# A two-layer encoder trunk on one core: separate PSUM banks and a fixed order at the stage borders, another beginning, and the pooling map moved one step forward

## The chip, the cores and the metric

The kernel runs on one core of one Trainium2 chip. The metric is the time of one execution on the device in microseconds (us); the median of three runs stands for a kernel. The engines named below are TensorE (PE, matrix products, with its weight loads PEld), VectorE (DVE), ScalarE (ACT), GpSimd (POOL) and SyncE (SP), which issues most of the transfers. PSUM is the memory that PE writes its results to; it has eight banks, each of 512 fp32 columns in 128 partitions.

## The reference

An input x of 256 tokens and 1024 channels passes two layers. Each layer does three things to it, all in fp32:

```
for l in range(2):
    x = x + 0.5 * swiglu(rmsnorm(x, ffn1_norm[l]), w_gate, w_up, w_down)     # 1024 -> 2816 -> 1024
    z = rmsnorm(x, mix_norm[l]) @ w_in[l]
    zq, zk, zv, zp, hq, hi, hff, hfb, hg = split(z)
    y_att  = dilated_attention(zq, zk, zv, ...)      # 8 heads of 64
    y_pool = pool_mixer(zp, pool_w[l], pool_scale[l])    # window means, a 64x64 map per group, a scale
    y_rec  = hgrn2_bidirectional(hq, hi, hff, hfb, hg, ...)
    x = x + concat(y_att, y_pool, y_rec) @ w_out[l]
    x = x + 0.5 * swiglu(rmsnorm(x, ffn2_norm[l]), w_gate, w_up, w_down)
```

The pooling map and its scale, `y_pool`, and the way x gets from one of the six stages to the next are what the change touches, beside the beginning.

## The kernel before, in words

**Products.** Each fp32 operand is split into a high part and a low part, and each product is three matmuls (high by high, low by high, high by low; lines 161 to 163 and 168 to 170). Weights come from memory in halves of 128x1024 (`stage`, SP's queue); ACT copies the high part (`whi`, line 149) and DVE subtracts to get the low part (`wlo`, line 150), four halves ahead of PE's use. One half feeds twelve matmuls of 512 columns or 24 of 256.

**Stages.** A layer is feed-forward 1, mixer, feed-forward 2. In a feed-forward, each of eleven blocks computes gate and up (`gu`), `g` on ACT and `h` on DVE, transposes h on PE (`hp`) and multiplies it into four accumulators `ya`, one for each half of the channels (dh) and of the tokens (tt). PE and SP follow the order of the program; ACT, DVE and POOL follow an order that a scheduler makes from it. In the mixer a table, ORDER, sets the order of steps: `c:n` takes a quarter chunk of the input projection, `rec` the recurrence's last products (`ops`), `sc`, `tr` and `pv` the attention, `pool` the pooling map (`pps`, then the parts `yh` on ACT and `yl` on DVE), and `o:` the output projection (`wo`), whose first part, `o:pool/0`, reads `yh` and `yl`.

**A border.** There are five borders, where a stage's result is added to x and becomes the next stage's input. At the end of a stage the last block of each (dh, tt) is a run of six matmuls; then DVE adds it to x (`add`, line 371), ACT sums its squares (`squares`, line 281), and, one run later, PE transposes that quarter of x by four transposes (`turn`, line 294) into PSUM tiles named `xps`. After both token halves ACT makes the high part `xh` (line 272) and DVE the low part `xl` (line 273) of each of four channel chunks k. An `xps` tile is one bank that holds two chunks. The last quarter's transposes are held back (`pending`) and run by `late_turn`: in a feed-forward ahead of the second weight half, in the mixer's first products (`proj_pair`) after 24 matmuls.

**PSUM.** The eight banks are two pools of four, `pg` (gate and up, hp, xps, most of the mixer's short-lived results) and `py` (the accumulators `ya`, and the output projection's).

**The beginning.** While the first transfers are under way PE does twelve idle products of a tile of ones; each is two passes in the trace. Then it transposes the first half of x, and the second half after the first weight half.

Of the kernel before, what the change touches and what calls it, by code (L numbers as in the profile page):

```python
# [16 lines left out]
P = 128  # L17
D = 1024
T = 256
KC = D // P  # L20
# [21 lines left out]
HALF = 1024  # L42
# [6 lines left out]
    (  # L49
# [4 lines left out]
    ),  # L54
    (
# [4 lines left out]
    ),  # L60
)
# [9 lines left out]
class Trunk:  # L71
    def __init__(self, ctx, tc, x_in, wall, prm_in, rel_in, cst_in, cst2_in, msk_in, band_in, y_out):
# [16 lines left out]
        self.n_split = 0  # L89
        self.cur = 0  # L90
        self.pending = self.then = None
        self.look = LOOK

        self.x = self.cp.tile([P, 2, D], F32, name="x")
# [27 lines left out]
        self.eps, self.one = (cols[:, n:n + 1] for n in range(2))  # L122
# [19 lines left out]
    def split_part(self, i, c0, c1):  # L142
        nc = self.nc
        self.feed_dma(i)
        if c0 == 0:
            self.split_t[i] = (self.whl.tile([P, HALF], F32R, tag="hi", name="whi"),
                               self.whl.tile([P, HALF], F32R, tag="lo", name="wlo"))
        (hi, lo), st, s = self.split_t[i], self.stage_t[i], slice(c0, c1)
        nc.scalar.activation(hi[:, s], st[:, s], AF.Copy)  # L149
        nc.vector.tensor_tensor(lo[:, s], st[:, s], hi[:, s].bitcast(F32), op=ALU.subtract)  # L150

    def ahead(self, i):

# [49 lines left out]
    def proj_pair(self, i0, accs, mid=None):  # L203

        self.ahead(i0)
        ws = [self.half(i0 + n, KC) for n in range(4)]
        order = [(kc, n) for kc in range(4) for n in range(4)] + [(kc, n) for n in range(4) for kc in range(4, KC)]
        for kc, n in order:
            if (kc, n) == (2, 0):
                self.late_turn()  # L210
            if (kc, n) == (KC - 1, 1) and mid is not None:
                mid()
            wh, wl = ws[n]
            self.mm3(accs[n // 2][:, n % 2, :], wh[:, kc, :], wl[:, kc, :], self.xh[:, kc, :], self.xl[:, kc, :],
                     start=(kc == 0 and n % 2 == 0), stop=(kc == KC - 1 and n % 2 == 1))
# [20 lines left out]
    def down(self, i, ys, ah, al, first, last, mid=None, post=None, dhs=(0, 1)):  # L236

        for dh in dhs:
            self.ahead(i + dh)
            wh, wl = self.half(i + dh, 2)  # L240
            for tt in range(2):
                s = slice(tt * P, tt * P + P)
                for f in range(2):
                    self.mm3t(ys[2 * dh + tt], ah[:, f, s], al[:, f, s], wh[:, f, :], wl[:, f, :],
                              start=(first and f == 0), stop=(last and f == 1))
                if post is not None:
                    post(dh, tt)
            if dh == 0 and mid is not None:
                mid()

# [11 lines left out]
    def new_xt(self):  # L262
# [2 lines left out]
        self.ss = self.wk.tile([P, 64], F32, tag="ss", name="ss", bufs=2)[:, 0:4]  # L265
        self.xps = {}

    def parts(self, stage, k, src):

        nc = self.nc  # L270
        g = self.prm[:, C_GAIN + stage * 8 + k:C_GAIN + stage * 8 + k + 1]
        nc.scalar.activation(self.xh[:, k, :], src, AF.Copy, scale=g)  # L272
        nc.vector.scalar_tensor_tensor(self.xl[:, k, :], src, g, self.xh[:, k, :].bitcast(F32),  # L273
                                       op0=ALU.mult, op1=ALU.subtract)

    def squares(self, stage, dh, tt):

# [9 lines left out]
    def turn(self, stage, dh, tt):  # L287

        nc = self.nc
        for j in range(4):  # L290
            k = 4 * dh + j
            if tt == 0 and j % 2 == 0:
                self.xps[k // 2] = self.pg.tile([P, 2, T], F32, tag="g", name="xps")
            nc.tensor.transpose(self.xps[k // 2][:, j % 2, tt * P:tt * P + P], self.x[:, tt, k * P:k * P + P], self.ident)  # L294
        if tt == 1:
            for k in range(4 * dh, 4 * dh + 4):
                self.parts(stage, k, self.xps[k // 2][:, k % 2, :])

    def rms(self, rows=False):

# [67 lines left out]

    def add(self, y, by, dh, tt, post):
        s = self.x[:, tt, dh * 512:dh * 512 + 512]  # L370
        self.nc.vector.scalar_tensor_tensor(s, y, by, s, op0=ALU.mult, op1=ALU.add)
        post(dh, tt)

    def to_stage(self, stage):
# [77 lines left out]
    def mixer(self, l):  # L452
# [4 lines left out]
        V = {}  # L457
# [4 lines left out]
        def bank(name):  # L462
            return pg.tile([P, 2, T], F32, tag="g", name=name)
# [281 lines left out]
            nc.scalar.activation(pm, ps, AF.Copy)  # L745

        def pool_out():
            ps = bank("pps")
            for n in range(2):
                c = C_PW + (2 * l + n) * P  # L750
                nc.tensor.matmul(ps[:, n, :], lhsT=self.prm[:, c:c + P], rhs=V["pm"][:, n, :], start=(n == 0),
                                 stop=(n == 1), skip_group_check=True)
            yh, yl = V["ypool"] = self.t2("yh", F32R), self.t2("yl", F32R)
            for n in range(2):
                sc = self.prm[:, C_PS + 2 * l + n:C_PS + 2 * l + n + 1]
                nc.scalar.activation(yh[:, n, :], ps[:, n, :], AF.Copy, scale=sc)
                nc.vector.scalar_tensor_tensor(yl[:, n, :], ps[:, n, :], sc, yh[:, n, :].bitcast(F32),
                                               op0=ALU.mult, op1=ALU.subtract)


# [51 lines left out]
    def body(self):  # L812
        nc = self.nc
        self.new_xt()

        idle = self.pg.tile([P, 512], F32, tag="g", name="idle")
        for _ in range(12):
            self.nc.tensor.matmul(idle[:, 0:P], lhsT=self.ones, rhs=self.ones, start=True, stop=True)
        for j in range(2):
            self.split_part(0, j * HALF // 2, (j + 1) * HALF // 2)  # L820
        self.n_split = 1
        for tt in range(2):
            self.turn(0, 0, tt)
        self.feed_dma(5)

        def second():
# [1 line left out]
                self.turn(0, 1, tt)  # L828

        def sums():  # L830
            for dh in range(2):
                for tt in range(2):
# [138 lines left out]
```

## Time and profile before

| | |
|---|---|
| median of three runs (lowest, highest) | 1016.76 us (1016.58, 1017.47) |
| profiled execution, its own time | 1017.16 us |
| its span | 1015.4 us |
| PE busy | 1002.1 us (99%) |
| DVE busy | 607.6 us (60%) |
| ACT busy | 539.2 us (53%) |
| granted clock of TensorE, mean | 0.999 |
| memory read | 179.15 MB |

The span runs from the first to the last instruction of the profiled execution; its own time is 1.8 us longer. A row of a timeline gives the start of an instruction in us from the span's start, how long it took (for x4, from the first one's start to the last one's end), its engine, line, operation and shape, and in brackets the idle time of the engine just before it with what ended it. Matmuls overlap: a matmul of 512 columns is shown with 0.39 us, but such matmuls start 0.23 us apart, so a busy engine can still be late, and a recorded wait is shorter than the time lost by it.

### The profile page before, as it was taken

Reading aid. Unit: us, or ns where it says so; the run is one execution under the profiler, and the core shown is the slowest. Engines: PE = TensorE matmul, PEld = TensorE weight load, DVE = VectorE, ACT = ScalarE, POOL = GpSimd, SP = SyncE. Lnnn points to the kernel's source line nnn. Section 1 sums busy time; section 2 is a strip of 40 time slices with the busy share of each in tenths; the row PEclk is TensorE's granted clock in tenths of the full one; section 3 lists DMA queues with packets and bytes.
Section 4 is the critical chain, followed back from the end, with each engine's and each line's share of the span. In section 5 each row is a group of like instructions: output and inputs, shape, how many; then the busy total and the mean of one; then the engine's idle time right before and its main releaser. Section 6 shows DMA issues by size and latency. Waiting matters only on the chain.

```text
span 1015.4 us, 14477 instructions
## 1 busy us (share of the span) xinstructions
PE 1002.1 (99%) x5722; PEld 827.2 (81%) x5722; DVE 607.6 (60%) x811; ACT 539.2 (53%) x774; POOL 3.3 (0%) x8
## 2 busy tenths in 40 slices
PE   9999999999999999999999999999999999999998
PEld 7888788798877888888878888888888778888886
DVE  5555555679865555555565454546998665545453
ACT  7444444675765544444474444446857764444441
POOL 0000100000000000000000000000000000000000
PEclk9999999999999999999999999999999999999999
DMA  7676775544434556555655565654553356555661
GB/s 265 216 259 189 265 271 187 170 163 147 127 104 146 184 186 190 187 187 186 188 165 188 187 188 186 189 185 144 186 154 117 106 146 186 188 187 187 189 189 56
DMA packets 50276, 181.16 MB, mean 178 GB/s; under 512 B 5752, under 2 KB 6008, under 8 KB 49952
## 3 DMA queue, kind: packets, MB, share of 16 engines
q1 hardware_dynamic: 48528, 174.09, 53.9%
q0 software_dynamic: 720, 4.21, 1.1%
q10 hardware_dynamic: 960, 1.94, 0.5%
q8 instruction: 45, 0.74, 0.3%
q14 instruction: 23, 0.19, 0.0%
HBM read 179.15 MB, written 3.16 MB: 180 GB/s over the span
## 4 chain that ended last, share of the span: by engine, by line
PE 93%; ACT 3%; DVE 3%; DMA 1%; issue 0%; SPq 0%; ACTq 0%
PE gu L168 16%; PE gu L170 16%; PE gu L169 16%; PE ya L170 8%; PE ya L168 8%; PE ya L169 8%; PE hp L352 2%; PE lev L544 1%; PE wo L168 1%; PE wo L170 1%; PE wo L169 1%; ACT whi L149 1%; DVE wlo L150 1%; PE zh L168 1%; PE xps L294 1%; PE pv L727 1%
## 5 line engine op out<-in xcount | busy, mean ns | idle before, releaser
L150 DVE TENSOR_TENSOR wlo<-stage,whi 128x1024 fp32r<-128x1024 f32 (+1 forms) x329 | 401.2, 1221 | 343.8 <-ACT whi L149 342.9
L149 ACT ACTIVATE whi<-stage 128x1024 fp32r<-128x1024 f32 (+1 forms) x329 | 347.3, 1057 | 373.2 <-PE gu L170 199.7
L168 PE MATMUL gu<-whi,xh 128*128 128x512 f32 x704 | 275.5, 391 | 3.5 <-DVE xl L273 2.2
L170 PE MATMUL gu<-whi,xl 128*128 128x512 f32 x704 | 274.3, 390 | 0.0
L169 PE MATMUL gu<-wlo,xh 128*128 128x512 f32 x704 | 274.0, 389 | 0.0
L168 PEld LDWEIGHTS gu<-whi,xh 128*128 128x128 f32 x704 | 132.1, 188 | 32.9 <-DVE xl L273 2.9
L170 PEld LDWEIGHTS gu<-whi,xl 128*128 128x128 f32 x704 | 132.1, 188 | 28.3 <-DVE xl L273 0.9
L169 PEld LDWEIGHTS gu<-wlo,xh 128*128 128x128 f32 x704 | 132.2, 188 | 27.0
L168 PE MATMUL ya<-whi,hi 128*128 128x512 f32 x352 | 141.5, 402 | 0.0
L170 PE MATMUL ya<-whi,lo 128*128 128x512 f32 x352 | 137.8, 391 | 0.0
L169 PE MATMUL ya<-wlo,hi 128*128 128x512 f32 x352 | 137.3, 390 | 0.0
L170 PEld LDWEIGHTS ya<-whi,lo 128*128 128x128 f32 x352 | 66.0, 188 | 14.4
L169 PEld LDWEIGHTS ya<-wlo,hi 128*128 128x128 f32 x352 | 66.3, 188 | 12.6
L168 PEld LDWEIGHTS ya<-whi,hi 128*128 128x128 f32 x352 | 66.2, 188 | 12.3
L345 ACT ACTIVATE g<-gu,rc 128x256 f32<-128x256 f32 x88 | 41.3, 474 | 46.6 <-PE gu L170 46.5
L346 DVE SCALAR_TENSOR_TENSOR h<-gu,rc,g 128x256 f32<-128x256 f32 x88 | 41.8, 480 | 23.4 <-ACT g L345 23.4
L258 DVE TENSOR_TENSOR lo<-hp,hi 128x512 fp32r<-128x512 f32 x44 | 30.1, 683 | 2.8 <-ACT hi L257 2.8
L257 ACT ACTIVATE hi<-hp 128x512 fp32r<-128x512 f32 x44 | 25.5, 580 | 2.7 <-PE hp L352 2.7
L352 PEld LDWEIGHTS hp<-cst,h 128*128 128x128 f32 x176 | 21.8, 139 | 5.7
L352 PE MATMUL hp<-cst,h 128*128 128x128 f32 x176 | 26.3, 271 | 0.0
L272 ACT ACTIVATE xh<-xps,prm 128x256 fp32r<-128x256 f32 x48 | 20.5, 469 | 5.9 <-DVE xl L273 3.4
L273 DVE SCALAR_TENSOR_TENSOR xl<-xps,prm,xh 128x256 fp32r<-128x256 f32 x48 | 21.3, 478 | 2.4 <-ACT xh L272 1.9
(223 smaller groups left out, 991.1 us busy)
## 6 DMA issues: line engine op xcount, KB each, us to landing
stage<-w_all SPq DMA_DIRECT2D x327, 512.0 KB, 3.5
skew<-drow POOLq DMA_DIRECT2D x1, 2048.0 KB, 11.2
bias<-skew POOLq DMA_DIRECT2D x2, 1024.0 KB, 11.2
x<-x SPq DMA_DIRECT2D x4, 256.0 KB, 4.9
band<-band ACTq DMA_DIRECT2D x1, 1024.0 KB, 8.3
y_t<-x SPq DMA_DIRECT2D x4, 256.0 KB, 2.2
stage<-w_all SPq DMA_DIRECT2D x2, 256.0 KB, 5.3
mskf<-msk ACTq DMA_DIRECT2D x1, 320.0 KB, 6.1
```

The lines of the kernel that those rows point to most:

```text
L149: nc.scalar.activation(hi[:, s], st[:, s], AF.Copy)
L150: nc.vector.tensor_tensor(lo[:, s], st[:, s], hi[:, s].bitcast(F32), op=ALU.subtract)
L168: nc.tensor.matmul(out, lhsT=ah, rhs=wh, start=start, stop=False, skip_group_check=True)
L169: nc.tensor.matmul(out, lhsT=ah, rhs=wl, start=False, stop=False, skip_group_check=True)
L170: nc.tensor.matmul(out, lhsT=al, rhs=wh, start=False, stop=stop, skip_group_check=True)
L257: self.nc.scalar.activation(hi, src, AF.Copy)
L258: self.nc.vector.tensor_tensor(lo, src, hi.bitcast(F32), op=ALU.subtract)
L272: nc.scalar.activation(self.xh[:, k, :], src, AF.Copy, scale=g)
L273: nc.vector.scalar_tensor_tensor(self.xl[:, k, :], src, g, self.xh[:, k, :].bitcast(F32), op0=ALU.mult, op1=ALU.subtract)
L345: silu = nc.scalar.activation(g2[:, tt, :], gu[tt][:, 0:256], AF.Silu, scale=r)
L346: nc.vector.scalar_tensor_tensor(h[:, tt, :], gu[tt][:, 256:512], r, g2[:, tt, :], op0=ALU.mult, op1=ALU.mult)
L352: nc.tensor.transpose(hp[:, f, tt * P:tt * P + P], h[:, tt, f * P:f * P + P], self.ident)
```

## The change

It has three parts.

**Borders.** The four chunks of the first half of x get a bank each in `pg`; those of the second half share two banks in `py`, k with k + 2. `parts` chains the instructions: each `xh` stands behind the `xh` before it on ACT, each `xl` behind the `xl` before it on DVE, and the squares behind the last `xh` issued. The low weight parts that fall due in a stage's last two runs are held and put behind the adds (0, 0) and (1, 1) on DVE. `proj_pair` does its first 24 matmuls on output parts 0 and 1 rather than on all four.

```
@@ split_part
-        nc.vector.tensor_tensor(lo[:, s], st[:, s], hi[:, s].bitcast(F32), op=ALU.subtract)
+        low = lambda: nc.vector.tensor_tensor(lo[:, s], st[:, s], hi[:, s].bitcast(F32), op=ALU.subtract)
+        if self.held is None:
+            low()
+        else:
+            self.held.append(low)
@@ proj_pair
-        order = [(kc, n) for kc in range(4) for n in range(4)] + [(kc, n) for n in range(4) for kc in range(4, KC)]
+        order = [(kc, 2 * p + e) for p in range(2) for kc in range(4) for e in range(2)] + [(kc, n) for n in range(4) for kc in range(4, KC)]
         for kc, n in order:
-            if (kc, n) == (2, 0):
+            if (kc, n) == (0, 2):
                 self.late_turn()
@@ down
+            self.held = [] if post is not None else None
             self.ahead(i + dh)
+            held, self.held = self.held, None
...
-                    post(dh, tt)
+                    added = post(dh, tt)
+                    if (dh, tt) in ((0, 0), (1, 1)):
+                        with self.tc.issue_after(added.ins):
+                            for low in held:
+                                low()
@@ parts
+    def behind(self, n):
+        return self.tc.issue_after(self.pins[n].ins) if self.pins[n] is not None else nullcontext()
...
+        with self.behind(0):
+            hi = nc.scalar.activation(self.xh[:, k, :], src, AF.Copy, scale=g)
+        with self.behind(1):
+            lo = nc.vector.scalar_tensor_tensor(self.xl[:, k, :], src, g, self.xh[:, k, :].bitcast(F32),
+                                                op0=ALU.mult, op1=ALU.subtract)
+        self.pins = [hi, lo]
@@ turn
-            if tt == 0 and j % 2 == 0:
-                self.xps[k // 2] = self.pg.tile([P, 2, T], F32, tag="g", name="xps")
+            if tt == 0 and dh == 0:
+                self.xps[k] = self.pg.tile([P, 2, T], F32, tag="g", name="xps")[:, 0, :]
+            elif tt == 0 and j < 2:
+                two = self.py.tile([P, 2, T], F32, tag="y", name="xps")
+                self.xps[k], self.xps[k + 2] = two[:, 0, :], two[:, 1, :]
...
+                if k == 2 and between is not None:
+                    between()
+                self.parts(stage, k, self.xps[k])
@@ to_stage
-            self.squares(stage, dh, tt)
             self.late_turn()
             self.pending = lambda: self.turn(stage, dh, tt)
+            with self.behind(0):
+                self.squares(stage, dh, tt)
```

On DVE, at the border from feed-forward 1 to the mixer in layer 0 (`x<-ya` is the add, `wlo` a low weight part, `xl` a chunk's low part), the kernel before has:

```order
L150 TENSOR_TENSOR wlo<-stage,whi 128x1024
L371 SCALAR_TENSOR_TENSOR x<-ya,x 128x512 x2
L150 TENSOR_TENSOR wlo<-stage,whi 128x1024
L371 SCALAR_TENSOR_TENSOR x<-ya,x 128x512
L273 SCALAR_TENSOR_TENSOR xl<-xps,prm,xh 128x256 x2
L371 SCALAR_TENSOR_TENSOR x<-ya,x 128x512
L273 SCALAR_TENSOR_TENSOR xl<-xps,prm,xh 128x256 x2
L150 TENSOR_TENSOR wlo<-stage,whi 128x1024
```

and the changed kernel:

```order
L396 SCALAR_TENSOR_TENSOR x<-ya,x 128x512
L152 TENSOR_TENSOR wlo<-stage,whi 128x1024
L396 SCALAR_TENSOR_TENSOR x<-ya,x 128x512 x2
L292 SCALAR_TENSOR_TENSOR xl<-xps,prm,xh 128x256 x4
L396 SCALAR_TENSOR_TENSOR x<-ya,x 128x512
L152 TENSOR_TENSOR wlo<-stage,whi 128x1024 x2
```

The first add now stands ahead of the low weight part, and the four low parts of x stand together ahead of the last add.

On ACT at the same border, with buffer numbers, before (`xps_1595` and `xps_1598` are banks of two chunks each):

```order
L149 ACTIVATE whi_1603<-stage_1499 128x1024
L281 ACTIVATE sq_1584,ss_1570<-x_83 128x512
L281 ACTIVATE sq_1593,ss_1570<-x_83 128x512
L272 ACTIVATE xh_1568<-xps_1595,prm_84 128x256
L272 ACTIVATE xh_1568<-xps_1598,prm_84 128x256
L281 ACTIVATE sq_1614,ss_1570<-x_83 128x512
L272 ACTIVATE xh_1568<-xps_1595,prm_84 128x256
L272 ACTIVATE xh_1568<-xps_1598,prm_84 128x256
```

and now (four banks):

```order
L301 ACTIVATE sq_1590,ss_1577<-x_83 128x512
L151 ACTIVATE whi_1612<-stage_1506 128x1024
L301 ACTIVATE sq_1608,ss_1577<-x_83 128x512
L290 ACTIVATE xh_1575<-xps_1600,prm_84 128x256
L290 ACTIVATE xh_1575<-xps_1602,prm_84 128x256
L290 ACTIVATE xh_1575<-xps_1604,prm_84 128x256
L290 ACTIVATE xh_1575<-xps_1606,prm_84 128x256
L301 ACTIVATE sq_1634,ss_1577<-x_83 128x512
```

Before, the third and fourth `xh` read the banks that the first two `xl` read; now each reads a bank of its own.

**The pooling map.** In both rows of ORDER the step `pool` moves from behind `rn2` to right behind `c:17`, and its two products get a bank each:

```
-        "... join c:17 rec rn1 sc:2 tr:2 tr:3 c:18 rn2 pool tr:4 tr:5 "
+        "... join c:17 pool rec rn1 sc:2 tr:2 tr:3 c:18 rn2 tr:4 tr:5 "
...
-            ps = bank("pps")
+            pps = [bank("pps")[:, 0, :] for _ in range(2)]
```

On ACT in layer 0, before:

```order
L149 ACTIVATE whi_2805<-stage_2520 128x1024
L613 ACTIVATE rrs_2771<-hss_2768,cols_106 128x512
L614 ACTIVATE rrs_2771<-rrs_2771 128x512
L682 ACTIVATE va_1798<-v_2628,rc_1733 128x512
L257 ACTIVATE hi_2776<-rrs_2771 128x512
L756 ACTIVATE yh_2783<-pps_2780,prm_84 128x256
L682 ACTIVATE va_1798<-v_2629,rc_1733 128x512
L717 ACTIVATE PT_2794<-tp_2789 128x512
L756 ACTIVATE yh_2783<-pps_2780,prm_84 128x256
L717 ACTIVATE PT_2801<-tp_2796 128x512
```

and now:

```order
L151 ACTIVATE whi_2771<-stage_2447 128x1024
L782 ACTIVATE yh_2694<-pps_2690,prm_84 128x256
L782 ACTIVATE yh_2694<-pps_2691,prm_84 128x256
L646 ACTIVATE sq_2717<-ops_2700 128x512
L270 ACTIVATE hi_2719<-sq_2717 128x512
```

The two `yh` have left the place among the recurrence's end (`rrs`, `hi`), the values (`va`) and the attention's transposed weights (`PT`), and stand ahead of the squares of `ops`.

**The beginning.** A copy of one column on ACT comes first (a table is loaded for it); the idle products are eight, two and six around the two groups of transposes; the first weight half's parts stand between the first two and the next two chunks' parts; and the four squares come behind all parts of x.

```
+        nc.scalar.activation(self.spare, self.one, AF.Copy)
+        warm(8)
+        self.turn(0, 0, 0)
+        warm(2)
+        self.turn(0, 0, 1, between=first)
+        warm(6)
...
         def sums():
-            for dh in range(2):
-                for tt in range(2):
-                    self.squares(0, dh, tt)
+            with self.behind(0):
+                for dh in range(2):
+                    for tt in range(2):
+                        self.squares(0, dh, tt)
```

ACT's first rows before, behind the two transfers that it issues:

```order
L281 ACT_TABLE_LOAD
L281 ACTIVATE sq,ss<-x 128x512
L149 ACTIVATE whi<-stage 128x512 x2
L272 ACTIVATE xh<-xps,prm 128x256 x2
L281 ACTIVATE sq,ss<-x 128x512
L272 ACTIVATE xh<-xps,prm 128x256
L281 ACTIVATE sq,ss<-x 128x512
L272 ACTIVATE xh<-xps,prm 128x256
L149 ACTIVATE whi<-stage 128x1024
```

and now (the first row of line 853 is the table's load):

```order
L853 ACT_TABLE_LOAD
L853 ACTIVATE cols<-cols 128x1
L290 ACTIVATE xh<-xps,prm 128x256 x2
L151 ACTIVATE whi<-stage 128x512 x2
L290 ACTIVATE xh<-xps,prm 128x256 x2
L151 ACTIVATE whi<-stage 128x1024 x2
L290 ACTIVATE xh<-xps,prm 128x256 x2
L151 ACTIVATE whi<-stage 128x1024
L290 ACTIVATE xh<-xps,prm 128x256
L151 ACTIVATE whi<-stage 128x1024
L290 ACTIVATE xh<-xps,prm 128x256
L301 ACTIVATE sq,ss<-x 128x512 x4
```

The parts of x now come ahead of the weight parts and of all squares; the four squares, a second table load, three weight parts, the two steps of `rc`, a further weight part and a third table load then come ahead of the first `g`.

## Rows read from the trace of the kernel before

The columns of a timeline are: start, length, engine, line, operation, output and inputs, shapes, count, and in brackets the idle time before with its releaser.

**Rows 1.** the page, busy time, share and instructions of each engine
```profile
PE 1002.1 (99%) x5722; PEld 827.2 (81%) x5722; DVE 607.6 (60%) x811; ACT 539.2 (53%) x774; POOL 3.3 (0%) x8
```

**Rows 2.** waits of PE: line, waited for: us in total, times, longest us
```profile
PE gu L168 <- DVE xl L273: 2.2, 3, 0.7
PE xps L294 <- DVE x L371: 1.6, 5, 0.3
PE ga L161 <- DVE xl L273: 1.5, 2, 0.7
PE wo L168 <- ACT yh L756: 1.1, 4, 0.6
```

**Rows 3.** timeline of PE, first border: start, length, line, [idle <-releaser]
```profile
193.75 0.39 PE L169 MATMUL ya<-wlo,hi 128*128 128x512 f32 x1
193.98 0.39 PE L170 MATMUL ya<-whi,lo 128*128 128x512 f32 x1
194.66 0.66 PE L294 MATMUL xps<-cst,x 128*128 128x128 f32 x4 [0.29 <-DVE x L371]
...
196.54 0.60 PE L294 MATMUL xps<-cst,x 128*128 128x128 f32 x4
196.89 0.48 PE L168 MATMUL ya<-whi,hi 128*128 128x512 f32 x1
...
198.37 0.60 PE L294 MATMUL xps<-cst,x 128*128 128x128 f32 x4
199.71 0.38 PE L161 MATMUL ga<-xh,whi 128*128 128x256 f32 x1 [0.74 <-DVE xl L273]
```

**Rows 4.** timeline of DVE, same border
```profile
192.78 1.23 DVE L150 TENSOR_TENSOR wlo<-stage,whi 128x1024 fp32r<-128x1024 f32 x1 [1.37 <-ACT whi L149]
193.92 1.28 DVE L371 SCALAR_TENSOR_TENSOR x<-ya,x 128x512 f32<-128x512 f32 x2
...
199.18 0.87 DVE L273 SCALAR_TENSOR_TENSOR xl<-xps,prm,xh 128x256 fp32r<-128x256 f32 x2
```

**Rows 5.** timeline of ACT, second half of the same border
```profile
204.27 0.86 ACT L272 ACTIVATE xh<-xps,prm 128x256 fp32r<-128x256 f32 x2 [0.34 <-DVE xl L273]
```

**Rows 6.** timeline of PE, output projection's beginning in both layers
```profile
292.03 0.39 PE L170 MATMUL v<-whi,xl 128*128 128x512 f32 x1
...
295.33 0.40 PE L168 MATMUL wo<-whi,yh 128*128 128x512 f32 x1
...
793.29 0.60 PE L715 MATMUL tp<-cst,P 128*128 128x128 f32 x4
...
796.33 0.40 PE L168 MATMUL wo<-whi,yh 128*128 128x512 f32 x1
```

**Rows 7.** timelines of ACT, DVE and PE around step rec of layer 0
```profile
282.81 0.60 ACT L619 ACTIVATE sq<-ops 128x512 f32<-128x512 f32 x1 [1.44 <-PE ops L599]
...
287.48 0.62 DVE L708 TENSOR_SCALAR P<-P,st 128x256 f32<-128x256 f32 x2
...
287.77 1.02 PE L751 MATMUL pps<-pm,prm 128*128 128x256 f32 x4
```

**Rows 8.** timelines of PE and ACT, the program's beginning
```profile
1.12 5.49 PE L818 MATMUL idle<-ones 128*128 128x128 f32 x24 [1.12 <-DVE ones L125]
...
27.25 0.60 PE L352 MATMUL hp<-cst,h 128*128 128x128 f32 x4
...
6.82 1.31 ACT L149 ACTIVATE whi<-stage 128x512 fp32r<-128x512 f32 x2 [1.71 <-DMA stage<-w_all]
...
8.75 0.63 ACT L281 ACTIVATE sq<-x 128x512 f32<-128x512 f32 x1
...
22.55 1.28 ACT L345 ACT_TABLE_LOAD   x1
23.85 0.84 ACT L345 ACTIVATE g<-gu,rc 128x256 f32<-128x256 f32 x2
...
27.45 1.06 ACT L149 ACTIVATE whi<-stage 128x1024 fp32r<-128x1024 f32 x1 [0.62 <-PE gu L170]
```

More of the change, by code (lines that the diff above doesn't have):

```diff
@@ L91, in __init__ @@
         self.pending = self.then = None
+        self.pins = [None, None]
+        self.held = None
         self.look = LOOK
@@ L121, in __init__ @@
         cols = self.cp.tile([P, 4], F32, name="cols")
-        self.eps, self.one = (cols[:, n:n + 1] for n in range(2))
+        self.eps, self.one, self.spare = (cols[:, n:n + 1] for n in range(3))
         nc.vector.memset(self.eps, EPS)
@@ L271, in parts @@
         g = self.prm[:, C_GAIN + stage * 8 + k:C_GAIN + stage * 8 + k + 1]
-        nc.scalar.activation(self.xh[:, k, :], src, AF.Copy, scale=g)
-        nc.vector.scalar_tensor_tensor(self.xl[:, k, :], src, g, self.xh[:, k, :].bitcast(F32),
-                                       op0=ALU.mult, op1=ALU.subtract)
+        with self.behind(0):
[4 more added lines that the diff above has]
+        self.pins = [hi, lo]
     def squares(self, stage, dh, tt):
@@ L285, in squares, with turn @@
                 nc.scalar.preload_act_table_set("natural_log_exp_and_others"))
-    def turn(self, stage, dh, tt):
+    def turn(self, stage, dh, tt, between=None):
         nc = self.nc
@@ L291, in turn @@
             k = 4 * dh + j
-            if tt == 0 and j % 2 == 0:
-                self.xps[k // 2] = self.pg.tile([P, 2, T], F32, tag="g", name="xps")
-            nc.tensor.transpose(self.xps[k // 2][:, j % 2, tt * P:tt * P + P], self.x[:, tt, k * P:k * P + P], self.ident)
+            if tt == 0 and dh == 0:
[3 more added lines that the diff above has]
+                self.xps[k], self.xps[k + 2] = two[:, 0, :], two[:, 1, :]
+            nc.tensor.transpose(self.xps[k][:, tt * P:tt * P + P], self.x[:, tt, k * P:k * P + P], self.ident)
         if tt == 1:
             for k in range(4 * dh, 4 * dh + 4):
-                self.parts(stage, k, self.xps[k // 2][:, k % 2, :])
+                if k == 2 and between is not None:
+                    between()
+                self.parts(stage, k, self.xps[k])
     def rms(self, rows=False):
@@ L370, in add @@
         s = self.x[:, tt, dh * 512:dh * 512 + 512]
-        self.nc.vector.scalar_tensor_tensor(s, y, by, s, op0=ALU.mult, op1=ALU.add)
+        added = self.nc.vector.scalar_tensor_tensor(s, y, by, s, op0=ALU.mult, op1=ALU.add)
         post(dh, tt)
+        return added
     def to_stage(self, stage):
         def post(dh, tt):
-            self.squares(stage, dh, tt)
             self.late_turn()
             self.pending = lambda: self.turn(stage, dh, tt)
+            with self.behind(0):
+                self.squares(stage, dh, tt)
         return post
@@ L747, in pool_out @@
         def pool_out():
-            ps = bank("pps")
+            pps = [bank("pps")[:, 0, :] for _ in range(2)]
             for n in range(2):
                 c = C_PW + (2 * l + n) * P
-                nc.tensor.matmul(ps[:, n, :], lhsT=self.prm[:, c:c + P], rhs=V["pm"][:, n, :], start=(n == 0),
-                                 stop=(n == 1), skip_group_check=True)
+                nc.tensor.matmul(pps[n], lhsT=self.prm[:, c:c + P], rhs=V["pm"][:, n, :], start=True, stop=True)
             yh, yl = V["ypool"] = self.t2("yh", F32R), self.t2("yl", F32R)
@@ L755, in pool_out @@
                 sc = self.prm[:, C_PS + 2 * l + n:C_PS + 2 * l + n + 1]
-                nc.scalar.activation(yh[:, n, :], ps[:, n, :], AF.Copy, scale=sc)
-                nc.vector.scalar_tensor_tensor(yl[:, n, :], ps[:, n, :], sc, yh[:, n, :].bitcast(F32),
+                nc.scalar.activation(yh[:, n, :], pps[n], AF.Copy, scale=sc)
+                nc.vector.scalar_tensor_tensor(yl[:, n, :], pps[n], sc, yh[:, n, :].bitcast(F32),
                                                op0=ALU.mult, op1=ALU.subtract)
@@ L814, in body, with warm, first @@
         self.new_xt()
[L816 to L820, printed above, removed]
+        idle = self.py.tile([P, 512], F32, tag="y", name="idle")
+        def warm(n):
+            for _ in range(n):
+                nc.tensor.matmul(idle[:, 0:P], lhsT=self.ones, rhs=self.ones, start=True, stop=True)
+        def first():
+            with self.behind(0), self.behind(1):
+                for j in range(2):
+                    self.split_part(0, j * HALF // 2, (j + 1) * HALF // 2)
+        nc.scalar.activation(self.spare, self.one, AF.Copy)
[4 more added lines that the diff above has]
+        warm(6)
         self.n_split = 1
-        for tt in range(2):
-            self.turn(0, 0, tt)
         self.feed_dma(5)
@@ L830, in sums @@
         def sums():
-            for dh in range(2):
-                for tt in range(2):
-                    self.squares(0, dh, tt)
+            with self.behind(0):
+                for dh in range(2):
+                    for tt in range(2):
+                        self.squares(0, dh, tt)
         self.pending, self.then, self.look = second, sums, 0
```

4 rows, old and new, of the table ORDER are left out of this document.

## Prediction

> **What bounds the kernel now.** I read the page's busy shares first: PE is busy for 1002.1 of 1015.4 us [rows 1], so time can only come out of the stretches in which PE is late, or out of fewer matmuls; the change removes none. Next the list of PE's waits [rows 2]: `xps` for the add of x five times, `gu` and `ga` together for `xl` five times, `wo` for `yh` four times. Five and five are the five borders, four is two for each layer's pooling map. The recorded waits sum to some 6 us, but they miss the tail of the matmul before, so I go to PE's timeline and measure each place against its due time, which is the start before it plus one step. Matmuls of 512 columns start 0.23 us apart (193.75 to 193.98) [rows 3].
>
> **Borders.** At the first border the last matmul ahead of the transposes starts at 193.98, so they are due at 194.21; they start at 194.66: 0.45 lost. Four transposes cost 0.35 (196.54 to 196.89). The last group starts at 198.37, so the mixer's first product is due at 198.72 and comes at 199.71: 0.99 lost [rows 3]. The other four borders show the same pair, with idle rows of 0.29 to 0.34 and 0.74: worked out in the same way they lose 0.50 + 0.97, 0.45 + 0.98, 0.45 + 0.97 and 0.50 + 0.97. The five sum to 7.2 us, and that is what the first part can remove.
>
> Does it? The first loss has its cause on DVE: a low weight part takes DVE from 192.78 to 193.92, and the add, whose matmuls were over at about 193.1, starts only then [rows 4]. In the new order the add stands first: about 193.1 to 193.75 (half of the 1.28 for two), ahead of 194.21. The held weight part (1.23, its step 1.14) then runs to about 194.9, and the second add, whose matmuls end near 194.8, to 195.55; its transposes are due at 194.21 + 1.88 = 196.1 (1.88 is the distance from 194.66 to 196.54 [rows 3]). A margin of 0.5 remains. The third add runs from 196.3 to 196.95, with its transposes due at 197.9.
>
> The second loss is a chain between ACT and DVE. Two chunks share a bank, and ACT's part of the one waits for DVE's part of the other, seen plainly in the second half: 0.34 idle, released by `xl` [rows 5]. Before, the last pair of `xl` starts at 199.18 [rows 4], and `ga` needs the first of the pair. With four banks ACT runs its four parts in one go, 0.42 each [rows 5], from 196.4 to 198.1; DVE follows its third add with four parts of 0.44 each [rows 4]: 197.4, 197.85, 198.3, 198.7. The next stage's first product is due at 194.21 + 1.88 + 1.83 + 0.35 = 198.3 (1.83 is the distance from 196.54 to 198.37 [rows 3]). It reads chunk 0, ready at 197.4; in the mixer `proj_pair` takes six matmuls a chunk (0.74 at 0.12 each), in a feed-forward the first weight half reads chunks 0 and 1 alone. Each chunk is there 0.5 us or more ahead. I take both losses as gone: −7.2. What now runs late is the pair of low weight parts behind the last add, to about 201.7; they are for weights three and four halves on (one half is 12 × 0.23 = 2.8 us), which hides them. Two banks of the second half lie in `py`, whose accumulators the adds have by then freed; the transposes wait for no other reader. If this cover were gone, the old 1.44 a border would be back, and no more unless an add is late too; bounds 0 to −7.2, and I take the lower end since every margin is 0.3 or more.
>
> **Pooling map.** In layer 0 the last product of v starts at 292.03, so the output projection is due at 292.26 and its seventh matmul at 292.26 + 6 × 0.23 = 293.64; it comes at 295.33: 1.69 lost. In layer 1 four transposes start at 793.29 (0.35), the projection is due at 793.64, its seventh matmul at 795.02, and it comes at 796.33: 1.31 lost [rows 6]. Together 3.0. The cause is that `yh` stands among the values, the attention's transposed weights and the recurrence's end on ACT. Moved ahead of the recurrence, the map's parts are ready some 9 us before their use, so the 3.0 go.
>
> Its price there: its four passes cost PE 0.86 (287.77 to 288.63 [rows 7], where the transposes begin), the same as in their old place. They push the recurrence and the scores `sc:2` back by 0.86, and give nothing back until `tr:4`. ACT has room: it was idle for 1.44 ahead of the squares of `ops` [rows 7], and two `yh` take about 0.8. The scores, now due at about 283.55, need the banks that `yl` reads; DVE does a low weight part until about 282.6 and then two `yl` of 0.44: ready at 283.4 to 283.5. Softmax is then 0.86 later as well: its last scaling, over at 288.1 [rows 7], comes at 288.95, and the transposes that read it, at 288.63 before, are now due behind the 0.23-us products at about the same place. Both margins are some 0.1 us, the thinnest of the change. Bounds: 0 to +1.1 a layer (two `yl` and their latency); I take 0, the end that these rows come out at.
>
> **Beginning.** [...]
>
> [...] Up to the third table load ACT has, from 6.9: eight `xh` of 0.40 (3.2), two half weight parts (1.2), eight whole ones of about 1.0 [rows 8] (8.0), four squares with their step of 0.61 [rows 8] (2.4), one table load (1.3), two `rc` (0.5) and some 0.8 of waiting for weights and transposes: 24.3. Before, that load started at 22.55. The load, and the two `g` behind it, end 24.69 − 22.55 = 2.14 later [rows 8], the last `h` (0.5) at about 27.0. So `hp` moves from 27.25 to 27.0: −0.25. [...] I take −0.25, where the sum comes out.
>
> **Sum.** 7.2 + 3.0 + 0.25 = 10.45 us. The profiled execution took 1017.16, its span 1015.4 with 1.8 outside, which the change leaves alone; so 1006.7 for that execution. The median of the runs is 0.4 lower, and from it I forecast 1006.3 us.
>
> **Rivals.**
> [...]
> (b) Only half of the border's loss goes, because the held weight part and the second add slip past the transposes' due time, or a later chunk is late. Then 3.6 + 3.0 + 0.25: 1009.9. For it: three DVE operations now stand in a row in the first half. Against it: the margins above.
> (c) The scores `sc:2` wait for the map's two banks, 1.1 in each layer: 1008.5. For it: the margin is 0.1.
> [...]
> (e) The waits are only renamed, and it doesn't do what it says: the add isn't early, since the scheduler's place is bound by something else. 1016.
>
> **Chances.** Forecast 0.60, own range 1005.3 to 1007.4; (a) 0.13; (b) 0.11; (c) 0.09; (d) 0.03; (e) 0.04. What can be told from no change is 0.2%, about 2 us. Faster is all of the forecast and (a) to (c): 0.93; the same 0.04; slower 0.03. The range takes in the forecast, (a) and (c) and most of (b): 1004.8 to 1010.0.
>
> **What would show it.** In the changed profile: no wait of `xps` for x nor of `gu` or `ga` for `xl` at a border, and 198.3 for `ga` in the first one (earlier by what the beginning gives); no wait of `wo` for `yh`; four `xh` in one row of ACT; the first `gu` near 8.35 and `hp` near 27.0. I am wrong if idle passes or the first `gu` run at 0.4 apart behind the transposes, if `sc` or `tp` waits behind the map, or if PE's waits for DVE come back under another name.

## The result, and the profile after

The changed kernel takes 1006.44 us (median of four runs, 1006.29 to 1006.98) against 1016.75 for the kernel before (four runs, 1016.58 to 1017.47): a ratio of 0.9898, 95% interval 0.9881 to 0.9915, so 10.3 us less. The forecast was 1006.3 in a range of 1004.8 to 1010.0. The profiled execution was the longest of the four: 1006.98, span 1005.2, while the other three have spans of 1004.5 to 1004.7.

The page's row of busy times, which answers to [rows 1]:

```profile
PE 998.3 (99%) x5730; PEld 828.1 (82%) x5730; DVE 605.2 (60%) x811; ACT 538.7 (54%) x775; POOL 3.3 (0%) x8
```

PE's share is 99% as before. Its busy time fell by 3.8 us and the span by 10.2: the other 6.4 had been recorded as idle time, and the 3.8 are the part of the losses that the tail of the matmul before had covered. The list of PE's waits, against [rows 2]:

```profile
PE idle L845 <- DVE ones L127: 1.1, 1, 1.1
PE gu L175 <- DVE wlo L152: 0.9, 2, 0.7
PE wo L174 <- ACT PT L744: 0.3, 1, 0.3
PE lev L571 <- DVE W L550: 0.2, 1, 0.2
```

None of the four waits of before is left. New are a wait for a low weight part at the beginning, and one of the output projection for ACT's copy `PT`. The first border on PE, against [rows 3]:

```profile
193.73 0.40 PE L176 MATMUL ya<-whi,lo 128*128 128x512 f32 x1
193.97 0.60 PE L317 MATMUL xps<-cst,x 128*128 128x128 f32 x4
...
195.80 0.60 PE L317 MATMUL xps<-cst,x 128*128 128x128 f32 x4
...
197.63 0.60 PE L317 MATMUL xps<-cst,x 128*128 128x128 f32 x4
197.99 0.36 PE L167 MATMUL ga<-xh,whi 128*128 128x256 f32 x1
```

From the last product ahead of the first transposes (193.73) to the next stage's first product (197.99) it is 4.26 us, nothing idle; before, it was 199.71 − 193.98 = 5.73. The other four borders go from 5.76, 5.73, 5.73 and 5.76 to 4.25, 4.25, 4.26 and 4.25. DVE and ACT there, against [rows 4, 5]:

```profile
192.80 0.69 DVE L396 SCALAR_TENSOR_TENSOR x<-ya,x 128x512 f32<-128x512 f32 x1 [1.63 <-PE ya L176]
193.41 1.22 DVE L152 TENSOR_TENSOR wlo<-stage,whi 128x1024 fp32r<-128x1024 f32 x1
194.54 0.69 DVE L396 SCALAR_TENSOR_TENSOR x<-ya,x 128x512 f32<-128x512 f32 x1
196.00 0.69 DVE L396 SCALAR_TENSOR_TENSOR x<-ya,x 128x512 f32<-128x512 f32 x1 [0.78 <-PE ya L176]
196.62 1.66 DVE L292 SCALAR_TENSOR_TENSOR xl<-xps,prm,xh 128x256 fp32r<-128x256 f32 x4
```

```profile
196.11 1.57 ACT L290 ACTIVATE xh<-xps,prm 128x256 fp32r<-128x256 f32 x4
```

The first add waits for PE alone and stands ahead of the weight part; the four low parts, and on ACT the four high parts, run in one go. The pooling map and the output projection, against [rows 6, 7]:

```profile
290.30 0.39 PE L176 MATMUL v<-whi,xl 128*128 128x512 f32 x1
...
291.88 0.39 PE L174 MATMUL wo<-whi,yh 128*128 128x512 f32 x1
...
785.27 0.60 PE L742 MATMUL tp<-cst,P 128*128 128x128 f32 x4
...
787.60 0.50 PE L174 MATMUL wo<-whi,yh 128*128 128x512 f32 x1 [0.33 <-ACT PT L744]
```

```profile
280.83 0.87 DVE L783 SCALAR_TENSOR_TENSOR yl<-pps,prm,yh 128x256 fp32r<-128x256 f32 x2
...
281.86 0.39 PE L719 MATMUL sc<-Hk,Hq 64*128 64x256 f32 x2
```

In layer 0 the seventh matmul comes 1.58 after the last one of v (3.30 before), which is its due time. In layer 1 it comes 2.33 after the transposes, 3.04 before, and still waits. `yl` is over at 281.70 and the scores start at 281.86 on time. The beginning, against [rows 8]:

```profile
1.11 3.78 PE L845 MATMUL idle<-ones 128*128 128x128 f32 x16 [1.11 <-DVE ones L127]
4.82 0.76 PE L317 MATMUL xps<-cst,x 128*128 128x128 f32 x4
5.42 0.61 PE L845 MATMUL idle<-ones 128*128 128x128 f32 x4
...
6.30 1.50 PE L845 MATMUL idle<-ones 128*128 128x128 f32 x12
7.58 0.50 PE L174 MATMUL gu<-whi,xh 128*128 128x512 f32 x1
8.31 0.49 PE L175 MATMUL gu<-wlo,xh 128*128 128x512 f32 x1 [0.23 <-DVE wlo L152]
...
26.73 0.85 PE L377 MATMUL hp<-cst,h 128*128 128x128 f32 x4
27.34 0.48 PE L174 MATMUL gu<-whi,xh 128*128 128x512 f32 x1
```

```profile
10.55 1.06 ACT L151 ACTIVATE whi<-stage 128x1024 fp32r<-128x1024 f32 x1 [1.77 <-DMA stage<-w_all]
...
24.30 1.28 ACT L370 ACT_TABLE_LOAD   x1
```

The twelve late idle passes take 1.28 us up to the next row, 0.107 each; the first sixteen took 3.71 up to the transposes (1.11 to 4.82), 0.232 each. The third table load stands at 24.30, and the first `gu` behind `hp` at 27.34 (27.60 before).

Put together along PE, from one landmark to the next: beginning 27.60 to 27.34, 0.26; five borders 28.71 to 21.27, 7.4; output projection's beginning 3.30 + 3.04 to 1.58 + 2.33, 2.4. That makes 10.1, and PE's last matmul starts at 1000.64 instead of 1010.79, 10.15 earlier.

### The profile page after: what moved, and what is told of

It is laid out like the page before. It is cut to its first block, busy times and chain, and to the rows that moved or that the text cites. A ratio compares the mean times of both kernels' runs of the same rounds, so it can differ in the third digit from the quotient of the medians.

```text
span 1005.2 us, 14482 instructions
## 1 busy us (share of the span) xinstructions
PE 998.3 (99%) x5730; PEld 828.1 (82%) x5730; DVE 605.2 (60%) x811; ACT 538.7 (54%) x775; POOL 3.3 (0%) x8
## 4 chain that ended last, share of the span: by engine, by line
PE 97%; DMA 1%; DVE 1%; ACT 1%; issue 0%; ACTq 0%
PE gu L175 16%; PE gu L176 16%; PE gu L174 16%; PE ya L176 8%; PE ya L174 8%; PE ya L175 8%; PE hp L377 2%; PE wo L174 2%; PE lev L571 1%; PE wo L175 1%; PE wo L176 1%; PE xps L317 1%; PE zh L174 1%; PE pv L754 1%; PE q L174 1%; PE zh L176 1%
```

## The experiments

Each edit is against the changed kernel unless it says otherwise. A median alone mixes two things, for the beginning varies from one execution to the next: with the same beginning, the first `gu` behind `hp` came at 27.34, 26.81, 26.88 and 27.94 (changed kernel, e5, e8, e9), and with the old one at 27.60 and 27.06 (kernel before, e2). So I also give the body: PE's last matmul minus that first `gu`. It is 983.19 before and 973.30 after. It comes from one execution of each kernel, but it repeats: where nothing behind the beginning differs from the changed kernel (e4, e10, e11) it is 973.22 to 973.27. The kernel before was timed again beside each group, with medians of 1016.70 (e1 to e4), 1016.75 (e5 to e8), 1017.10 (e9 to e11) and 1016.58 (e12); the changed kernel was not, so a difference of medians from it is uncertain by some of these 0.5 us.

**e1, borders alone.** Beginning and pooling map as before, the border part kept:

```
-        "... c:17 pool rec rn1 sc:2 ... c:18 rn2 tr:4 "
+        "... c:17 rec rn1 sc:2 ... c:18 rn2 pool tr:4 "
-        warm(8)
-        self.turn(0, 0, 0)
-        warm(2)
-        self.turn(0, 0, 1, between=first)
-        warm(6)
+        for _ in range(12):
+            self.nc.tensor.matmul(idle[:, 0:P], lhsT=self.ones, rhs=self.ones, start=True, stop=True)
+        for j in range(2):
+            self.split_part(0, j * HALF // 2, (j + 1) * HALF // 2)
...
+        for tt in range(2):
+            self.turn(0, 0, tt)
```

> The border part alone (own banks, chained parts, held low weight parts, the other product order), beginning and pooling map as before. My account: all of the border loss of 7.2 us goes and nothing else changes, so about 1009.6 us, with the first ga at 198.3 and no wait of xps, gu or ga. Rival, the parts share one gain (the waits overlap, each part alone gets less, or one part brings nearly all): this run comes out at 1007 or at 1012 or more.

Measured 1008.43 (1008.15 to 1008.87; before 1016.70): 8.3 less. The body is 975.61, 7.6 less: my 7.2 and a little. The rest is in the beginning. Its order is the old one, but the border part's banks and chained parts reach it too:

```profile
7.39 1.55 ACT L290 ACTIVATE xh<-xps,prm 128x256 fp32r<-128x256 f32 x4
```

```profile
26.05 0.60 PE L377 MATMUL hp<-cst,h 128*128 128x128 f32 x4
```

With a bank each, ACT makes the first four `xh` in one go (before it made two, then one, then one, between squares), and `hp` comes at 26.05.

**e2, pooling map alone** (the ORDER and `pps` edits on the kernel before):

```
+        "... c:17 pool rec rn1 sc:2 ... c:18 rn2 tr:4 "
+            pps = [bank("pps")[:, 0, :] for _ in range(2)]
```

> The pooling part alone (step moved, two banks). My account: 3.0 us less, 1013.8, no wait of wo for yh, and scores not late. Rival, the stall comes back one step on: the attention's product pv waits for PT or va, which were hidden by the old stall, and only 1 to 2.5 us go: 1014.3 to 1015.8.

1014.29 (1014.09 to 1014.75; before 1016.70), 2.4 less; body 980.83, also 2.4 less. The rival was right in kind and size: in layer 1 a stall of 0.6 remains, which the old one had covered. It is not at `pv`, as the rival had it, but at the projection's seventh matmul:

```profile
793.30 0.50 PE L168 MATMUL wo<-whi,yh 128*128 128x512 f32 x1 [0.33 <-ACT PT L717]
```

**e3, beginning alone.** Borders and pooling map as before, two chunks a bank:

```
-            if tt == 0 and dh == 0:
-                self.xps[k] = self.pg.tile([P, 2, T], F32, tag="g", name="xps")[:, 0, :]
-            elif tt == 0 and j < 2:
-                two = self.py.tile([P, 2, T], F32, tag="y", name="xps")
-                self.xps[k], self.xps[k + 2] = two[:, 0, :], two[:, 1, :]
+            if tt == 0 and j % 2 == 0:
+                two = self.pg.tile([P, 2, T], F32, tag="g", name="xps")
+                self.xps[k], self.xps[k + 1] = two[:, 0, :], two[:, 1, :]
-        self.pins = [hi, lo]
+        self.pins = [hi, lo] if stage == 0 else [None, None]
```

(with the hold, the product order and the squares' place as before)

> The beginning alone. Here the scheduler puts nine whole weight parts, not eight, ahead of the third table load on ACT. My account, that the first hp waits for h and h for ACT's row of work: one part more (1.0) makes hp end 1.0 later than in the changed kernel, so about 0.75 slower than before: 1017.5, with the table's load at about 25.3. Rival, PE's own stream sets the end of the first block: 0.5 to 1.0 faster than before, 1016.0.

1019.75 (1018.79 to 1020.16; before 1016.70): 3.05 slower, and all of it ahead of the first `hp`, since the body is 983.17, that of before. The sign is that of my account, and `hp` does wait 0.83 for h, but the size and most of its cause aren't mine: chained in the order of the chunks, two of which share a bank, each second part waits for the other engine.

```profile
7.87 0.47 ACT L290 ACTIVATE xh<-xps,prm 128x256 fp32r<-128x256 f32 x1 [0.55 <-DVE xl L292]
...
27.52 1.28 ACT L368 ACT_TABLE_LOAD   x1
```

ACT waits so twice (0.55, and 0.46 at 15.85), PE's transposes once (0.61), and a weight that ACT waits 1.35 for lands late; the third table load comes at 27.52, where I had 25.3. So the new order at the beginning, chained as it is here, needs the new banks.

**e5, banks alone.** At the borders only the banks are new:

```
-            self.held = [] if post is not None else None
+            self.held = None
-        self.pins = [hi, lo]
+        self.pins = [hi, lo] if stage == 0 else [None, None]
-        order = [(kc, 2 * p + e) for p in range(2) for kc in range(4) for e in range(2)] + ...
+        order = [(kc, n) for kc in range(4) for n in range(4)] + ...
```

> The changed kernel, but at the borders only the banks are new: no held weight parts, no chained parts, old product order. Theory A, banks cure the second loss and the order the first: the first loss comes back, 5 x 0.47 = 2.4 us, 1008.8, waits of xps for x at five borders, none of gu or ga for xl. Theory B, the order does both: 7.2 back, 1013.6.

1009.32 (1009.04 to 1009.43): 2.9 more than the changed kernel. Body 975.89, 2.6 more. The five borders take 4.73 to 4.80 each, 0.5 more, all of it ahead of the first transposes; theory A. At the first border the weight part stands ahead of the first add again:

```profile
191.99 1.23 DVE L152 TENSOR_TENSOR wlo<-stage,whi 128x1024 fp32r<-128x1024 f32 x1 [1.38 <-ACT whi L151]
193.13 1.28 DVE L396 SCALAR_TENSOR_TENSOR x<-ya,x 128x512 f32<-128x512 f32 x2
```

```profile
193.87 0.66 PE L317 MATMUL xps<-cst,x 128*128 128x128 f32 x4 [0.29 <-DVE x L396]
```

The run undoes the hold of the weight parts, the chains, the product order and the squares' place together. That the hold is what cures the first loss is read from these rows, not tested alone; and since the second loss stays away with the banks alone, no run shows that the chains or the product order bring anything at a border.

**e6, old banks, new orders.**

```
-            if tt == 0 and dh == 0:
-                self.xps[k] = self.pg.tile([P, 2, T], F32, tag="g", name="xps")[:, 0, :]
-            elif tt == 0 and j < 2:
-                two = self.py.tile([P, 2, T], F32, tag="y", name="xps")
-                self.xps[k], self.xps[k + 2] = two[:, 0, :], two[:, 1, :]
+            if tt == 0 and j % 2 == 0:
+                two = self.pg.tile([P, 2, T], F32, tag="g", name="xps")
```

> The changed kernel with the old banks (two chunks a bank, all in pg), the orders new. Theory A, the banks' sharing decides the second loss: 4 to 5 us back, 1010.5 to 1011.5, waits of gu or ga for xl. Theory B, the order alone is enough: under 0.5 us back, 1006.9 or less.

1015.74 (1015.09 to 1015.98), worse than I had it. The beginning of e3 is in it (`gu` behind `hp` at 30.34, 3.0 later). The body is 979.15, 5.9 more than the changed kernel. At a border into a feed-forward:

```profile
322.82 0.60 PE L315 MATMUL xps<-cst,x 128*128 128x128 f32 x4
323.48 0.50 PE L174 MATMUL gu<-whi,xh 128*128 128x512 f32 x1
...
326.09 0.47 PE L174 MATMUL gu<-whi,xh 128*128 128x512 f32 x1 [0.95 <-DVE xl L292]
```

```profile
322.43 0.84 ACT L290 ACTIVATE xh<-xps,prm 128x256 fp32r<-128x256 f32 x2 [0.55 <-DVE xl L292]
```

The first loss is gone (transposes are on time at all five borders), but ACT waits 0.55 for `xl` between two chunks of a bank, the next stage's first product comes 0.66 behind the last transposes rather than 0.35 (at all five), and the second `gu` waits 0.95 for the last `xl`. Theory A in kind and somewhat more in size. The matmul that waits 0.95 reads `xh`, not `xl`: what it needs of DVE is the bank that its result takes over.

**e7, where the second half lies.** As e5, but two chunks share a bank; only the second half's two banks are taken from `py`:

```
+            if tt == 0 and j % 2 == 0:
+                two = (self.py if dh else self.pg).tile([P, 2, T], F32, tag="y" if dh else "g", name="xps")
+                self.xps[k], self.xps[k + 1] = two[:, 0, :], two[:, 1, :]
```

> As e5, but two chunks share a bank as before; only the second half's two banks lie in py. Theory A1, the next stage's first product waits because its result takes over the bank that the first two chunks are read from (rotation of four): with two banks fewer in the rotation it takes another, and most of the second loss goes; with the first loss back and up to 0.4 for a late second chunk at three borders: 3.6 us back, 1010. Theory A2, two chunks in one bank make the parts themselves late: all 7.2 back, 1013.6.

1011.20 (1011.03 to 1011.46); body 976.06, within 0.2 of e5, its borders 4.73 to 4.81. What e7 loses against e5 beyond that is the beginning (`gu` behind `hp` at 28.75). At the first border:

```profile
199.50 0.60 PE L315 MATMUL xps<-cst,x 128*128 128x128 f32 x4
199.85 0.36 PE L167 MATMUL ga<-xh,whi 128*128 128x256 f32 x1
```

```profile
199.70 0.69 DVE L394 SCALAR_TENSOR_TENSOR x<-ya,x 128x512 f32<-128x512 f32 x1 [0.21 <-PE ya L176]
200.31 0.87 DVE L292 SCALAR_TENSOR_TENSOR xl<-xps,prm,xh 128x256 fp32r<-128x256 f32 x2
```

`ga` starts at 199.85, right behind the transposes, while DVE has not yet begun the last pair of `xl` (200.31). In the kernel before, it waited for that pair's first [rows 3, 4], though it reads `xh`, not `xl`, and though the pair ahead had been over for 1.4 us:

```profile
197.46 0.88 DVE L273 SCALAR_TENSOR_TENSOR xl<-xps,prm,xh 128x256 fp32r<-128x256 f32 x2
```

So the second loss was no lack of data: the result of `ga` took over, in the rotation of four banks, the one that the pair was still read from. A1 holds.

**e8, pooling map moved, one bank.**

```
-            pps = [bank("pps")[:, 0, :] for _ in range(2)]
+            ps = bank("pps")
+            pps = [ps[:, n, :] for n in range(2)]
```

> The changed kernel with the pooling map moved but its two products in one bank. If the margin at the scores is as thin as 0.1 us, the second yh has to wait for the first yl, the bank is free 0.5 later and the scores wait 0.3 to 0.5 in each layer: 1007.1. Rival, the scores' banks are others than the map's: no change, 1006.4.

1006.94 (1006.67 to 1007.27), 0.5 more than with two banks; the body, 973.92, is 0.6 more. The second `sc` waits:

```profile
281.95 0.38 PE L719 MATMUL sc<-Hk,Hq 64*128 64x256 f32 x1 [0.16 <-DVE yl L785]
```

It comes at 281.95 where the matmul before it started at 281.41: some 0.4 late, in both layers. In exchange the projection's seventh matmul in layer 1 is nearly on time (787.77 against 786.29 for the first). The thin margin was there, and the second bank keeps it.

**e9, old place, two banks.**

```
-        "... c:17 pool rec rn1 sc:2 ... c:18 rn2 tr:4 "
+        "... c:17 rec rn1 sc:2 ... c:18 rn2 pool tr:4 "
```

> The changed kernel with the pooling map in its old place but two banks. My account, that its place on ACT's row costs 3.0: 2 to 3 us back, 1008.4 to 1009.4, waits of wo for yh or yl. Rival, that the sharing of one bank by yh and yl made the loss: under 1 us back, 1007.2.

1009.79 (1009.37 to 1010.24), 3.35 more; the body 975.95, 2.65 more. The size is that of my account, the place isn't:

```profile
288.61 0.70 PE L778 MATMUL pps<-pm,prm 128*128 128x256 f32 x2 [1.42 <-ACT rrs L640]
```

No product waits for `yh` any more. The map's second bank is the one that ACT's `rrs` still reads, and PE stands 1.42 in each layer. A second bank in the old place only moves the stall.

**e10, no idle products; e11, transposes in their place.** The three removed lines are both runs' edit, the added ones e11's alone, behind both groups of transposes:

```
-        warm(8)
...
-        warm(2)
...
-        warm(6)
+        for _ in range(24):
+            nc.tensor.transpose(idle[:, 0:P], self.x[:, 0, 0:P], self.ident)
```

> The changed kernel without the sixteen idle products; PE then works first on the transposes of x. If the early work is what lifts the clock's level, the first products of gu start 0.4 us apart for some while, and it costs what these are late: 6 to 12 matmuls by 0.21 = 1.3 to 2.5 us, of which about 1.0 hides behind the wait for the second low weight part: 0.3 to 1.5, 1006.7 to 1008. Rival, the level is there anyway: 0.23 apart from the first, 1006.4.

> The changed kernel with no idle products, but 24 further transposes of one chunk of x ahead of the first product (their results are not used). If transposes lift the clock as products do, the later of them take half the time of the first, and gu starts at about 9.5 at 0.23 apart: with q0 some 1.9 later and 1.0 of it hidden, 1006.5 to 1007.5. [...]

e10 took 1009.02 (1008.66 to 1009.61), e11 1008.57 (1007.85 to 1009.21). Their bodies are 973.27 and 973.22, so it is all in the beginning. In e10 the first weight half's products are 0.43 apart up to 12.90, then 0.23:

```profile
10.34 0.63 PE L174 MATMUL gu<-whi,xh 128*128 128x512 f32 x1
10.77 0.63 PE L175 MATMUL gu<-wlo,xh 128*128 128x512 f32 x1
...
14.77 0.40 PE L174 MATMUL gu<-whi,xh 128*128 128x512 f32 x1
15.01 0.40 PE L175 MATMUL gu<-wlo,xh 128*128 128x512 f32 x1
```

That is 12 × 0.2 = 2.4 us, and little of it hides: `gu` behind `hp` is at 29.47, 2.1 later than in the changed kernel's profile, more than the 1.5 I had as the upper end (1.5 to 2.7 later than in the four executions of the changed kernel's beginning given above). In e11 (`q0` in its expectation is the first weight half) the second product starts 0.32 behind the first and the third 0.23 behind the second; the next are 0.23 apart too:

```profile
6.04 1.12 PE L317 MATMUL xps<-cst,x 128*128 128x128 f32 x4 [0.44 <-DMA x<-x]
6.95 4.44 PE L857 MATMUL idle<-cst,x 128*128 128x128 f32 x24
11.14 0.47 PE L174 MATMUL gu<-whi,xh 128*128 128x512 f32 x1
11.46 0.39 PE L175 MATMUL gu<-wlo,xh 128*128 128x512 f32 x1
11.69 0.40 PE L176 MATMUL gu<-whi,xl 128*128 128x512 f32 x1
```

The 24 transposes take 4.19 us, 0.175 each, between the 0.23 of the four right ahead of them (6.04 to 6.95) and the 0.10 of eight in the changed kernel (10.97 to 11.76). So in this execution, with 32 transposes and no product ahead of it, the first weight half ran at 0.23; in e10, with eight transposes ahead of it, it ran at 0.43 up to 12.90. e11's median lies 1.07 above the 1007.5 that I had as the upper end, and the first `gu`, at 11.14 where I had about 9.5, comes 3.6 later than in the changed kernel because the 24 transposes stand ahead of it.

**e4 and e12, another beginning, and the stall in layer 1.** e4 puts two squares and the second weight half's parts right behind the transposes:

```
-        self.n_split = 1
+        with self.behind(0):
+            for tt in range(2):
+                early = self.squares(0, 0, tt)
+        with self.tc.issue_after(early.ins):
+            for j in range(2):
+                self.split_part(1, j * HALF // 2, (j + 1) * HALF // 2)
+        self.n_split = 2
```

The last two squares stay where they were. e12 adds, in layer 1:

```
-        "... c:18 rn2 tr:3 tr:4 c:19 tr:5 o:pool/0 ... "
+        "... c:18 rn2 tr:3 tr:4 tr:5 c:19 o:pool/0 ... "
```

> The changed kernel with the first two squares put into ACT's idle 1.8 us at the beginning, and the second weight half split into two parts of 512 columns. My account: ACT's row up to h is 1.1 shorter, the wait for the second low weight part (0.7) goes, and the first block ends 1.1 us earlier: 1005.3. Rival, the weights' transfers or the order on ACT set the pace: at most 0.3 less, 1006.1, and ACT idle again ahead of a weight part.

> As e4, and in layer 1 the step tr:5 stands ahead of c:19, so that all three of ACT's copies PT come ahead of the second va. In e4 as in the changed kernel PE loses 0.6 us there: the third run of the output projection takes over a bank that PT still reads. My account: PT is over 0.7 earlier, the 0.6 goes, 1005.4, no wait of wo for PT in layer 1. Rival, the earlier transposes wait for the softmax instead: the wait moves to tp and nothing is gained, 1006.0.

e4 took 1005.99 (1005.81 to 1006.46): 0.45 less than the changed kernel, between the two expectations and nearer the rival's. Its `hp` came at 25.62 and its body is 973.22, unchanged. e12 took 1005.63 (1005.40 to 1005.83; ratio to before 0.9892, interval 0.9875 to 0.9908). Its body is 972.67, 0.55 less than e4's, as expected:

```profile
786.51 0.43 PE L174 MATMUL wo<-whi,yh 128*128 128x512 f32 x1
```

The seventh matmul comes 1.36 after the first, with no wait for `PT`. The runs of e12 lie below all of the changed kernel's (1006.29 and up), so it beats both kernels; its 0.8 us are less than 0.1%, and as the two were not timed side by side I take it as likely, not as settled.

## Why the prediction was right, and where its reasons were not

**What bounds the kernel.** Right: PE's late starts were all there was to win, and reading them against due times gave 10.2 us where the recorded waits gave some 6.

**Borders, −7.2 forecast, −7.4 measured.** Right in size. The first loss had the cause I gave: with the orders undone together it is back, 0.5 at each border, and the weight part stands ahead of the add (e5). The second was put down to a chain of ACT and DVE over shared banks that makes the parts late. That step was wrong in its cause. e7 keeps the sharing and the old order and loses nothing there; what waited was the next stage's result for its bank. That the size came out all the same is luck in part: with a bank for each chunk, the tile that the rotation gives to the next stage's first result had held one early chunk alone, a reason that the prediction did not have. The parts' order matters only together with the banks: chained by chunk over shared banks it is worse (e6). `ga` came where it was worked out, at 197.99 against 198.3 − 0.3.

**Pooling map, −3.0 forecast, −2.4 measured.** The move does it, and the scores and the transposes wait for nothing; with one bank they wait (e8), so rival (c) was near: `yl` was over 0.16 ahead of the scores. Mis-sized was the term for layer 1: −1.3, measured −0.7. I took the whole stall as gone without asking what was late next: the projection's seventh matmul begins its second run of six and comes 0.6 late, in e2 and in the changed kernel alike. It waits for ACT's `PT`, which it does not read, so what it needs is the bank that `PT` is copied from; moving one step of transposes ends the wait (e12). I also took the place alone for the cause; e9 shows that the second bank would not have worked in the old place.

**Beginning, −0.25 forecast, −0.26 measured.** The table load came at 24.30, as summed, but by terms that cancel: ACT began its first `xh` at 6.17, not 6.9, and waited 2.0 for transfers (1.77 and 0.20), not 0.8. No run shows the 6.9, an estimate of mine, that this sum starts from and that the 8.35 for the first `gu` rests on: in its place the runs show 6.17, and 6.84 in e3. And the spread between executions is larger than the term, so that the sum agrees to 0.01 is luck. The first `gu` was early (7.58, not 8.35), and its second matmul waited for the low weight part (8.31), which the prediction did not have; the next weight half waited too. And the step named the wrong reason: with the old order and the new banks (e1) `gu` behind `hp` came at 26.41, with the new order and the new banks between 26.81 and 27.94. e1 is one execution, so what the new order costs beside the banks stays open; that it brings something isn't shown by any run. The medians less the body say the same: 33.5 before, 33.1 in the changed kernel (33.0 to 33.8 in e5, e8 and e9) and 32.8 in e1.

**The rivals.** (a) and (d), 0.13 and 0.03, were the cases of a beginning, or of whole blocks, at the slow pace, and fell in the changed profile itself: late passes 0.107 apart, products of the first weight half 0.23 apart from 8.64 on. e10, where these are 0.43 apart up to 12.90, gives the price of a slow first weight half: some 2 us. (b) did not come, since all five borders are on time; e5 shows its size, 2.6. (c) did not come either, but by 0.16 only. (e) is ruled out by the list of waits.

**The sum.** The three parts by themselves give −8.3, −2.4 and +3.05, together −7.65 against −10.3 for the whole. The parts do not add, since the banks of the first are what the third needs. Behind the beginning they do: the bodies fall by 7.6, 2.4 and 0.0, together 10.0, and by 9.9 for the whole. The median lies 0.14 from the forecast, closer than the parts: the pooling map's term was 0.6 too large, the borders' 0.2 too small, and the beginning alone varies by 1.1 among the four executions above.

## What to carry to other kernels

A wait named after a reader may be a wait for the reader's bank, as the 0.74 of `ga` was [rows 3]: before reordering work, ask which buffer the waiting instruction writes and who had it last. When a stall is taken away, the next in line is found by moving everything behind it forward by its length and looking who then comes late. Test the parts of a change apart and together: here one part was a loss without another.

## What the runs showed of the hardware

The record's granted clock reads 1.00 in each of four stretches of e10 from 4.40 to 16.00, while matmuls of 512 columns there start 0.43 apart from 8.64 to 12.90 and 0.23 apart from 14.54 on: at this program's beginning the pace is to be read from the spacing. PE had done eight transposes and twelve products, from 4.41 on, before the spacing fell.

The same work took different times there: twenty-four idle passes 5.49 us in the kernel before, 5.02 in e1 and 4.31 in e2. With the changed kernel's beginning the first `gu` came at 7.58, 7.74, 8.09 and 8.30 (changed kernel, e5, e8, e9). The `gu` behind `hp` did not follow that order (27.34, 26.81, 26.88, 27.94); it went with ACT's first whole weight part, which waited for its transfer in all four: 10.55, 9.97, 9.86 and 10.55. So where the transfers land is the likelier source of the beginning's spread; no run tests it alone.
